# Two mask copies of the gated attention on ScalarE, and the root iterations of both norm tails on GpSimd

## The chip, the cores and the metric

One NeuronCore of a Trainium2 chip runs the kernel. Time is device microseconds (us) of one launch on that core; the number compared is the median of several runs. The engines are TensorE (PE in the profile, PEld for its weight loads), VectorE (DVE), ScalarE (ACT), GpSimd (POOL) and SyncE (SP), which issues most transfers. Each engine takes its own instructions strictly in order and waits for the others through semaphores.

## The reference, cut to what matters

One encoder layer runs over a prompt of 1024 frames and a sample of 64 frames, in float32. The change touches the two attentions and the norm that follows each of them.

```python
def _head_groupnorm(o):                      # after retention
    mu = jnp.mean(o, axis=-1, keepdims=True)
    var = jnp.mean(jnp.square(o - mu), axis=-1, keepdims=True)
    return (o - mu) * lax.rsqrt(var + EPS)

def _head_rms(o):                            # after gated linear attention
    return o * lax.rsqrt(jnp.mean(o * o, axis=-1, keepdims=True) + EPS)

def _gla(q, k, v, log_a, s0):
    ...
        rel = jnp.where(causal, b[:, :, :, None, :] - b[:, :, None, :, :], -jnp.inf)
        att = jnp.einsum('bhtd,bhsd,bhtsd->bhts', qc, kc, jnp.exp(rel))
        o = inter + jnp.einsum('bhts,bhse->bhte', att, vc)
...
    o_r = _merge(_head_groupnorm(o_r)) * g_ret_norm.astype(f32) * jax.nn.silu(rg)
    o_g = _merge(_head_rms(o_g)) * g_gla_norm.astype(f32) * jax.nn.silu(gr)
```

## The kernel before

The 1088 frames are cut into three column blocks of 384, 384 and 320, each of up to three groups of 128 frames. All projections are made as three float32r products (high by high, low by high, high by low) that accumulate in a PSUM tile called `mm`. First comes the head of the program (norm, conditioning, first projections), then the gated attention (two passes, one for each pair of heads, about 120 to 330 us), then retention (four heads, about 345 to 600 us), then the output projection and the ConvFFN, which the change leaves alone.

**The gated attention.** `gla(p, c0)` goes through the three blocks of one head pair. I call the work of one block a *stretch*; six of them follow one another. A stretch fills the score tile `att`, of which there is one buffer, in seven levels (`LEVELS` = 64, 32, 16, 8, 4, 2, 1) after a diagonal step. For a level of width c, `pre1` has GpSimd subtract (`dd`) and ScalarE take exponentials, `pre2` makes `kk` (GpSimd or VectorE) and `qbd` (VectorE), and `fin` has TensorE multiply them into a PSUM tile `sc` of two buffers, from which VectorE copies the valid part into `att` under an integer mask `tmask` (`copy_predicated`). After the levels come three outputs: TensorE makes `o` from `att`, the values and the state `sbd`; VectorE updates `sbd`, which the next output needs; ScalarE copies `o` into `on` and sums its squares.

**The tails.** When a block's outputs are out, a tail is started as a side task: `gla_tail` scales `on` by the reciprocal root of the mean square, transposes it on TensorE and writes it into `mix`. `ret_tail` does the same for a retention head and block, with mean and variance from `bn_stats`. The reciprocal root is made from integer tricks and three Newton iterations by `rsqrt_steps`, on VectorE: two integer operations and nine small operations on 128 x 6 (gated, tiles `ga`, `gr`) or 128 x 3 elements (retention, `ra`, `rr`). There are 6 gated and 12 retention tails. `ons` has one buffer in the gated attention and two in retention.

**What sets the order.** Nothing reorders instructions on the chip. While the program is written out, a planner keeps a model clock (`Flow`, `flow.t`) that each matmul moves forward, and side tasks (generators: `gla`, `ret`, the tails, `mod_pieces`) are resumed when the clock has passed their due time. `Engine` keeps a modelled backlog of each engine (`behind()`); a level's `pre1` waits while GpSimd or ScalarE is more than `LEVEL_LIMIT` behind, and `mod_pieces` (multiply-adds `acc` of the conditioning weights, off to the side) go in whenever VectorE is less than `VECTOR_LIMIT` behind. So a change in how much work an engine is charged moves levels, tails and `acc` operations to other places between the projection matmuls. When the projections that a pass has are used up, `flow.drain` lets the clock jump, and what is left of the pass is written with no projections in between.

Of the kernel before, what the change touches and what calls it, by code (L numbers as in the profile page):

```python
# [12 lines left out]
F32 = mybir.dt.float32  # L13
F32R = mybir.dt.float32r
I32 = mybir.dt.int32
AF = mybir.ActivationFunctionType
ALU = mybir.AluOpType
PSUM = bass.MemoryType.PSUM

P = 128  # L20
# [4 lines left out]
CW = 384  # L25
# [168 lines left out]
def stream_step_kernel(  # L194
# [130 lines left out]
                actp.tile([P, CW], F32R, tag="act", name="act_lo"))  # L325

    smallp = [small]

    def rsqrt_steps(v, n, tag, out, w=P):
        ii = smallp[0].tile([P, n], I32, tag=tag + "i", name=tag + "i", bufs=2)[0:w]  # L330
# [413 lines left out]
    op = order.op  # L744
# [195 lines left out]
    def gla(p, c0):  # L940
# [66 lines left out]
        def fin(c, o):  # L1007
            q, k = qk[p, "q"][c], qk[p, "k"][c]
            if o == "diag":
                for hd in range(2):  # L1010
                    r = slice(hd * 64, hd * 64 + 64)
                    pd = bank(ps_sc, "sc")
                    for j in range(3):
                        sl = slice(j * P, (j + 1) * P)
                        mm(pd[:, sl], k[r, sl], q[r, sl], True, True)
                    V.copy_predicated(
                        out=att[:, :, hd, :],
                        mask=tmask[:, 0:P][:, None, :].broadcast_to([P, 3, P]),
                        data=pd[:, 0:CW].rearrange("p (j t) -> p j t", t=P))
            elif o == "kh":  # L1020
                kh = live.pop((c, "kh"))
                pk = bank(ps_sc, "sc")
                for j in range(3):
                    tr(pk[:, j * P:(j + 1) * P], kh[:, j * P:(j + 1) * P])
                khT = live[c, "khT"] = attn.tile([P, CW], F32, tag="kT", name="khT", bufs=2)
                S.copy(out=khT, in_=pk[:, 0:CW])
            elif isinstance(o, int):
                cc = LEVELS[o]
                kk, z = live.pop((c, "z", o))
                pl = bank(ps_sc, "sc")  # L1030
                for j in range(3):
                    mm(pl[:, j * P:(j + 1) * P], kk[:, j * P:(j + 1) * P],
                       z[:, j, :, :].rearrange("p h t -> p (h t)"), True, True)
                ao = att.rearrange("p j h (n two t) -> p (j h) n two t", two=2, t=cc)
                mo = 128 + 64 * o
                V.copy_predicated(
                    out=ao[:, :, :, 1, :],
                    mask=tmask[:, mo:mo + 64].rearrange("p (n t) -> p n t", t=cc)[:, None, :, :]
                    .broadcast_to([P, 6, 64 // cc, cc]),
                    data=pl[:, 0:CW].rearrange("p (g n t) -> p g n t", g=6, t=cc))  # L1040
            elif o != "qe":
                j = o[1]
                if j == 0:
                    live[c, "on"] = (ons.get(),
                                     small.tile([P, 6], F32, tag="gss", name="gss", bufs=2))
                on, ss = live[c, "on"]
                v, qe, khT, eL = vts[c0][c], live[c, "qe"], live[c, "khT"], live[c, "eL"]
                gi = c * 3 + j
                sst = cur["s"] if gi < 8 else sbd[2]
                sl = slice(j * P, (j + 1) * P)  # L1050
                po = bank(ps_o, "o")
                pst = po[:, 256:512]
                if sst is not None:
                    mm(po[:, 0:256], qe[:, sl], sst.rearrange("p h e -> p (h e)"), True, False)
                for hd in range(2):
                    mm(po[:, hd * P:(hd + 1) * P], att[:, j, hd, :], v[:, j, hd * P:(hd + 1) * P],
                       sst is None, sst is None or hd == 1)
                mm(pst, khT[:, sl], v[:, j, :], True, True)
                ns = sbd[gi % 2]
                for hd in range(2):  # L1060
                    r = slice(hd * 64, hd * 64 + 64)
                    if sst is None:
                        V.tensor_copy(out=ns[r, hd, :], in_=pst[r, hd * P:(hd + 1) * P])
                    else:
                        V.scalar_tensor_tensor(out=ns[r, hd, :], in0=sst[r, hd, :],
                                               scalar=eL[r, j:j + 1],
                                               in1=pst[r, hd * P:(hd + 1) * P], op0=ALU.mult,
                                               op1=ALU.add)
                S.copy(out=on[:, j, :, :], in_=po[:, 0:256])
                for hd in range(2):  # L1070
                    junk = small.tile([P, P], mybir.dt.bfloat16, tag="junk", name="junk", bufs=2)
                    S.activation(out=junk, in_=on[:, j, hd, :], func=AF.Square,
                                 accum_out=ss[:, 2 * j + hd:2 * j + hd + 1])
                cur["s"] = ns
                if gi >= 7:
                    dst = o_gla_p if gi == 7 else o_gla_s
                    for hd in range(2):
                        nc.sync.dma_start(out=dst[0, 0, 2 * p + hd],
                                          in_=ns[hd * 64:hd * 64 + 64, hd, :])
                if j == 2:  # L1080
                    vs.free()
                    tails_.append(flow.start(gla_tail(p, c, on, ss), 1.0))
# [37 lines left out]
    def gla_tail(p, c, on, ss):  # L1120
# [1 line left out]
        ms = small.tile([P, 6], F32, tag="ms", name="ms", bufs=2)  # L1122
        V.tensor_scalar(out=ms, in0=ss, scalar1=1.0 / P, scalar2=EPS, op0=ALU.mult, op1=ALU.add)
        rs = []
        for _ in rsqrt_steps(ms, 6, "g", rs):
            yield 0.2
        rs = rs[0]
        yield 0.2
        for j in range(3):
            for hd in range(2):  # L1130
                i = 2 * j + hd
# [167 lines left out]
    def ret_tail(hd, c, on, mv):  # L1299
        w = WID[c]  # L1300
        ve = small.tile([P, 3], F32, tag="ve", name="ve", bufs=2)
        V.tensor_scalar(out=ve, in0=mv[:, :, 1], scalar1=EPS, scalar2=None, op0=ALU.add)
        rs = []
        for _ in rsqrt_steps(ve, 3, "r", rs):
            yield 0.2
        rs = rs[0]
        yield 0.2
        for j in range(3):
            V.tensor_scalar(out=on[:, j, :], in0=on[:, j, :], scalar1=mv[:, j, 0:1],
                            scalar2=rs[:, j:j + 1], op0=ALU.subtract, op1=ALU.mult)  # L1310
        yield max(V.behind(), 0.0) + RET_TAIL
        pt = bank(ps_sc, "sc")
        for j in range(3):
            tr(pt[:, j * P:(j + 1) * P], on[:, j, :])
        mt = mix[c][hd]
        if mt is None:
            S.activation(out=new_mix(c, hd)[:, 0:w], in_=pt[:, 0:w], func=AF.Copy,
                         scale=vec("gret", hd))
        else:
            V.scalar_tensor_tensor(out=mt[:, 0:w], in0=pt[:, 0:w], scalar=vec("gret", hd),  # L1320
                                   in1=mt[:, 0:w], op0=ALU.mult, op1=ALU.mult)
        rons.free()
        ready[c] += 1
# [1033 lines left out]
```

## Time and profile before

| | |
|---|---|
| median of 3 runs | 1491.79 us (1491.54 to 1493.49) |
| the profiled execution | 1496.77 us, of which 1495.0 us are its span |
| mean granted TensorE clock | 0.97 of full speed |
| busy share PE / DVE / ACT / POOL | 92% / 72% / 42% / 21% |
| gated attention, 120 to 345 us | PE busy 195.98 of 225 us |
| retention, 345 to 612 us | PE busy 243.64 of 267 us |

The profile shows one execution, read by the hardware profiler, with its own time; it is 5.0 us above the median of the three runs. "Busy" counts an instruction from start to end, with what it waits inside. An idle time is given with the instruction of another engine whose end released it. L91 is the line of the planner's helper that issues every VectorE, ScalarE and GpSimd operation, and L234 and L239 issue the matmuls and the transposes, so tiles tell the groups apart.

### The profile page before, as it was taken

What the parts mean: (1) busy time and instruction counts of PE and PEld (TensorE: products, weight loads), DVE (VectorE), ACT (ScalarE), POOL (GpSimd) and SP (SyncE); (2) the same over time, 40 slices, a digit from 0 to 9 for tenths busy, and PEclk for the clock granted to TensorE, in tenths of its full rate; (3) what the DMA queues carried; (4) which work ended last, traced back from release to release, by engine and by line L of the source; (5) the groups of instructions that cost most, each with busy time, mean ns of one, the idle gap of its engine ahead of it and who ended that gap; (6) DMA issues with size and microseconds to landing.
All of it is one profiled execution on the core that took longest, in us unless ns stands there. A gap on an engine that the chain in (4) does not pass through costs nothing.

```text
span 1495.0 us, 23802 instructions
## 1 busy us (share of the span) xinstructions
PE 1372.2 (92%) x9082; PEld 1277.3 (85%) x9082; DVE 1070.9 (72%) x1992; ACT 625.8 (42%) x1277; POOL 307.2 (21%) x412
## 2 busy tenths in 40 slices
PE   5999888989999998799779999999999999899996
PEld 3788777879988988798769999999999997788875
DVE  6637878967886788646697777777777765568775
ACT  5735434432333223435464444444434444334343
POOL 3335423415242323411110000000000011110010
PEclk9999999999999999899889999999999999999998
DMA  8420102123222222444302422333233338565522
GB/s 255 155 76 4 55 15 75 45 84 100 83 79 86 76 75 62 118 149 139 104 15 72 140 60 76 107 106 98 95 99 106 106 100 289 185 195 184 173 81 113
DMA packets 157977, 158.27 MB, mean 106 GB/s; under 512 B 9738, under 2 KB 128616, under 8 KB 157864
## 3 DMA queue, kind: packets, MB, share of 16 engines
q1 hardware_dynamic: 147303, 120.58, 26.1%
q0 software_dynamic: 10560, 36.18, 7.1%
q8 instruction: 71, 1.16, 0.3%
q14 instruction: 43, 0.34, 0.1%
HBM read 126.80 MB, written 29.93 MB: 105 GB/s over the span
## 4 chain that ended last, share of the span: by engine, by line
PE 56%; DVE 22%; issue 8%; ACT 6%; DMA 2%; POOL 1%; DVEq 0%; ACTq 0%; POOLq 0%
PE dX L234 23%; PE mm L234 10%; PE dA L234 8%; PE mn L234 5%; PE al L234 3%; PE o L234 2%; DVE lo L91 2%; DVE qbd L91 2%; DMA rb<-d_y 2%; DVE acc L91 2%; DVE att L91 1%; ACT hi L91 1%; DVE X L91 1%; PE sc L234 1%; DVE ab L91 1%
## 5 line engine op out<-in xcount | busy, mean ns | idle before, releaser
L234 PE MATMUL dX<-X,lo 128*128 128x272 f32 x1344 | 182.0, 292 | 5.5 <-DVE ab L91 3.4
L234 PEld LDWEIGHTS dX<-X,lo 128*128 128x128 f32 x1344 | 175.6, 191 | 6.6 <-ACT cv L91 3.0
L234 PE MATMUL dX<-X,hi 128*128 128x272 f32 x1296 | 174.8, 291 | 5.0 <-DVE ab L91 2.8
L234 PEld LDWEIGHTS dX<-X,hi 128*128 128x128 f32 x1296 | 168.7, 191 | 5.8 <-issue 2.9
L234 PE MATMUL mm<-act_hi,hi 128*128 128x384 f32 (+1 forms) x480 | 170.8, 356 | 0.3 <-DVE mix L91 0.2
L234 PE MATMUL mm<-act_lo,hi 128*128 128x384 f32 (+1 forms) x480 | 158.9, 331 | 0.1
L234 PE MATMUL mm<-act_hi,lo 128*128 128x384 f32 (+1 forms) x480 | 158.5, 330 | 0.0
L91 ACT CAST hi<-raw 128x512 fp32r<-128x512 f32 (+1 forms) x116 | 91.1, 787 | 78.9 <-DVE raw L91 66.7
L234 PE MATMUL al<-ba,hi 128*128 128x512 f32 x396 | 102.1, 401 | 4.8 <-DVE x L91 4.8
L234 PE MATMUL mn<-lo,hi 128*128 128x512 f32 x396 | 94.6, 395 | 2.7 <-ACT lo L91 2.1
L234 PEld LDWEIGHTS mm<-act_hi,hi 128*128 128x128 f32 x480 | 92.1, 192 | 1.9 <-DVE mix L91 0.5
L234 PEld LDWEIGHTS mm<-act_lo,hi 128*128 128x128 f32 x480 | 91.9, 191 | 0.7 <-POOL act_lo L91 0.3
L234 PEld LDWEIGHTS mm<-act_hi,lo 128*128 128x128 f32 x480 | 91.4, 190 | 0.0
L234 PEld LDWEIGHTS mn<-lo,hi 128*128 128x128 f32 x396 | 74.7, 190 | 19.4 <-ACT lo L91 2.6
L91 DVE SCALAR_TENSOR_TENSOR cv<-ab,cw,cv 128x1088 f32<-128x1088 f32 x44 | 59.3, 1347 | 44.3 <-ACT cv L91 44.3
L234 PEld LDWEIGHTS al<-ba,hi 128*128 128x128 f32 x396 | 72.3, 191 | 20.0 <-DVE x L91 5.9
L234 PE MATMUL mm<-hi,act_hi 128*128 128x256 f32 x288 | 88.3, 307 | 0.3 <-ACT hi L91 0.2
L234 PE MATMUL mm<-lo,act_hi 128*128 128x256 f32 x288 | 82.7, 287 | 3.0 <-DVE lo L91 3.0
L234 PE MATMUL mm<-hi,act_lo 128*128 128x256 f32 x288 | 82.1, 285 | 0.0
L91 POOL TENSOR_TENSOR acc<-acc,prod 128x512 f32<-128x512 f32 x42 | 64.8, 1544 | 81.6 <-ACT prod L91 80.8
L234 PE MATMUL dA<-X,hi 128*128 128x272 f32 x552 | 74.3, 291 | 0.0
L234 PEld LDWEIGHTS dA<-X,hi 128*128 128x128 f32 x552 | 71.8, 191 | 0.0
(352 smaller groups left out, 3091.7 us busy)
## 6 DMA issues: line engine op xcount, KB each, us to landing
raw<-in_w_ffn_in_dram SPq DMA_DIRECT2D x44, 512.0 KB
raw<-in_w_ada_dram SPq DMA_DIRECT2D x32, 512.0 KB
raw<-in_w_in_dram SPq DMA_DIRECT2D x28, 512.0 KB
rw<-in_w_ffn_out_dram SPq DMA_DIRECT2D x51, 256.0 KB
d_y<-cv POOLq DMA_DIRECT2D x22, 512.0 KB, 4.8
rb<-d_y POOLq DMA_DIRECT2D x44, 256.0 KB, 3.8
raw<-in_w_out_dram SPq DMA_DIRECT2D x18, 512.0 KB
wa<-in_w_ada_dram SPq DMA_DIRECT2D x16, 512.0 KB
```

The costliest lines, as they stand in the source:

```text
L91: return call(*args, **kw)
L234: T.matmul(out, lhsT, rhs, start=start, stop=stop, skip_group_check=more)
```

## The change

Two things change in `gla` and the tails. For the two widest levels, `fin` no longer calls `copy_predicated` on VectorE: ScalarE copies the valid rectangles, which need no mask (one copy of 64 x 6 x 64 elements for width 64, two of 32 x 6 x 32 for width 32). And both tails use `root_steps` instead of `rsqrt_steps`: the two integer operations stay on VectorE, back to back, and each of three iterations is four GpSimd operations in place of three on VectorE. The tails yield 0.5 between iterations (0.2 between single operations before), and afterwards until the modelled GpSimd backlog is over.

```diff
+    def root_steps(v, n, tag, out):
+
+        def part(name, dt=F32, bufs=2):
+            return small.tile([P, n], dt, tag=tag + name, name=tag + name, bufs=bufs)
+
+        ii, jj = part("i", I32), part("j", I32)
+        V.tensor_scalar(out=ii, in0=v.bitcast(I32), scalar1=1, scalar2=None,
+                        op0=ALU.logical_shift_right)
+        V.tensor_scalar(out=jj, in0=ii, scalar1=-1, scalar2=0x5F3759DF,
+                        op0=ALU.mult, op1=ALU.add)
+        r = jj.bitcast(F32)
+        G.after(V)
+        for it in range(3):
+            yield
+            a = part("a")
+            G.tensor_tensor(out=a, in0=r, in1=r, op=ALU.mult)
+            G.tensor_tensor(out=a, in0=a, in1=v, op=ALU.mult)
+            G.tensor_scalar(out=a, in0=a, scalar1=-0.5, scalar2=1.5, op0=ALU.mult, op1=ALU.add)
+            r2 = part("r", bufs=3)
+            G.tensor_tensor(out=r2, in0=r, in1=a, op=ALU.mult)
+            r = r2
+        out.append(r)
@@ in gla, fin(c, o), one of the levels
+                if o < 2:
+
+                    for n in range(64 // cc):
+                        r = slice(2 * cc * n, 2 * cc * n + cc)
+                        S.copy(out=att[r, :, :, 2 * cc * n + cc:2 * cc * (n + 1)],
+                               in_=pl[r, 0:CW].rearrange("p (j h t) -> p j h t", j=3, h=2)
+                               [:, :, :, cc * n:cc * (n + 1)])
+                    return
                 ao = att.rearrange("p j h (n two t) -> p (j h) n two t", two=2, t=cc)
@@ in gla_tail (and the same in ret_tail, with ve, 3 and "r")
-        for _ in rsqrt_steps(ms, 6, "g", rs):
-            yield 0.2
+        for _ in root_steps(ms, 6, "g", rs):
+            yield 0.5
         rs = rs[0]
-        yield 0.2
+        yield max(G.behind(), 0.2)
```

The order of the instructions moves with it. On TensorE, the end of the last gated stretch: the last level (`qbd`, `kk`), then the outputs (`sbd` with `qe`, `v` with `att`, `v` with `khT`), with projection matmuls (`mm`) among them. Before:

```order
L234 MATMUL sc<-qbd_1079,kk 128x128 x3
L234 MATMUL mm<-act_hi,hi 128x384
L234 MATMUL mm<-act_lo,hi 128x384
L234 MATMUL mm<-act_hi,lo 128x384
L234 MATMUL o<-sbd_1083,qe 128x256
L234 MATMUL o<-v,att 128x128 x2
L234 MATMUL o<-v,khT 128x256
L234 MATMUL mm<-act_hi,hi 128x384
L234 MATMUL mm<-act_lo,hi 128x384
L234 MATMUL mm<-act_hi,lo 128x384
L234 MATMUL o<-sbd_1081,qe 128x256
L234 MATMUL o<-v,att 128x128 x2
```

Now, from the same level to the tail's transposes (`sc<-ident,on`):

```order
L234 MATMUL sc<-qbd_1079,kk 128x128 x3
L234 MATMUL o<-sbd_1083,qe 128x256
L234 MATMUL o<-v,att 128x128 x2
L234 MATMUL o<-v,khT 128x256
L234 MATMUL o<-sbd_1081,qe 128x256
L234 MATMUL o<-v,att 128x128 x2
L234 MATMUL o<-v,khT 128x256
L234 MATMUL o<-sbd_1085,qe 128x256
L234 MATMUL o<-v,att 128x128 x2
L234 MATMUL o<-v,khT 128x256
L234 MATMUL st<-ident,acc_2927 128x128 x4
L239 MATMUL sc<-ident,on 128x128 x6
```

Before, projections stand between the outputs, and 45 more of them between the last output and the tail's transposes; now there are none in either place. They stand further ahead, in the earlier stretches.

On VectorE, in the second retention head: between the outputs' updates (`rstate`, `on`, `bst`, `bmv`) stand the root iterations of the tail one block back (`ra`, `rr`), and `on<-on,bmv,rr` ends it. Before:

```order
L91 SCALAR_TENSOR_TENSOR rr<-ra,rj 128x3
L91 SCALAR_TENSOR_TENSOR ra<-ve,rr 128x3
L91 TENSOR_TENSOR ra<-ra,rr 128x3
L91 SCALAR_TENSOR_TENSOR rr<-ra,rr 128x3
L91 SCALAR_TENSOR_TENSOR rstate<-rstate,o 128x128
L91 SCALAR_TENSOR_TENSOR on<-o,txi,on 128x128
L91 BN_STATS bst<-on 128x6
L91 BN_AGGR bmv<-bst 128x2
L91 SCALAR_TENSOR_TENSOR ra<-ve,rr 128x3
L91 SCALAR_TENSOR_TENSOR acc_4357<-raw,csil,acc_4357 128x512
L91 TENSOR_TENSOR ra<-ra,rr 128x3
L91 SCALAR_TENSOR_TENSOR rr<-ra,rr 128x3
```

Now, at the same place, up to the end of the tail:

```order
L91 TENSOR_TENSOR mix<-mix,gate 128x384
L91 SCALAR_TENSOR_TENSOR acc_4532<-raw,csil,acc_4532 128x512
L91 SCALAR_TENSOR_TENSOR rstate<-rstate,o 128x128
L91 SCALAR_TENSOR_TENSOR on<-o,txi,on 128x128
L91 BN_STATS bst<-on 128x6
L91 BN_AGGR bmv<-bst 128x2
L91 TENSOR_SCALAR on<-on,bmv,rr 128x128 x3
L91 TENSOR_TENSOR ratt<-sc,tdec 128x384
```

The small operations are gone from VectorE. On GpSimd, they now stand between the additions `acc<-acc,prod` of a conditioning piece, each of which waits for a product that ScalarE makes:

```order
L91 TENSOR_TENSOR acc_4533<-acc_4533,prod 128x512
L91 TENSOR_TENSOR ra<-rj 128x3
L91 TENSOR_TENSOR ra<-ra,ve 128x3
L91 TENSOR_SCALAR ra<-ra 128x3
L91 TENSOR_TENSOR rr<-rj,ra 128x3
L91 TENSOR_TENSOR acc_4533<-acc_4533,prod 128x512
```

Before, GpSimd had only the additions there.

## Rows read from the trace of the kernel before

**Rows 1.** Windows: length; PE, PEld, DVE, ACT, POOL busy; clock; DMA share, GB/s.

```profile
131.50:165.30 33.80, 27.75 (x174) 26.01 (x173) 28.50 (x53) 10.73 (x32) 14.46 (x14) 0.90 0.16 48
165.30:196.10 30.80, 26.09 (x166) 23.37 (x165) 24.12 (x52) 12.90 (x44) 12.80 (x13) 1.00 0.11 35
196.10:229.50 33.40, 29.25 (x190) 26.59 (x189) 28.35 (x57) 14.23 (x51) 11.64 (x14) 0.95 0.09 25
229.50:260.40 30.90, 25.96 (x193) 24.51 (x192) 25.24 (x55) 11.47 (x39) 12.62 (x14) 0.94 0.17 50
260.40:289.90 29.50, 26.86 (x197) 24.66 (x196) 26.51 (x55) 13.64 (x47) 11.64 (x12) 1.00 0.17 53
289.90:331.00 41.10, 35.65 (x218) 32.17 (x217) 30.01 (x69) 17.01 (x55) 12.38 (x12) 0.96 0.27 85
361.00:612.00 251.00, 229.68 (x1560) 222.23 (x1558) 188.86 (x479) 84.56 (x174) 85.59 (x71) 0.97 0.24 73
```

**Rows 2.** Waits, 120 to 345 us: total, times, longest.

```profile
PE sc L234 <- DVE att L91: 13.5, 11, 3.7
...
PE o L234 <- DVE sbd L91: 3.4, 9, 0.6
```

**Rows 3.** Waits, 345 to 610 us.

```profile
PE sc L239 <- DVE on L91: 10.2, 5, 3.1
...
PE o L234 <- DVE rstate L91: 4.1, 4, 1.5
```

**Rows 4.** Groups, VectorE, 120 to 345 us (roots: first, last of six).

```profile
L91 DVE COPY_PREDICATED att<-tmask,sc 128x384 f32<-128x384 int32 x54 | 35.9, 677 | 8.2 <-PE sc L234 7.4
...
L91 DVE SCALAR_TENSOR_TENSOR gr<-ga,gr 128x6 f32<-128x6 f32 x12 | 4.9, 407 | 0.4
...
L91 DVE SCALAR_TENSOR_TENSOR gr<-ga,gj 128x6 f32<-128x6 f32 x6 | 1.7, 290 | 0.0
```

**Rows 5.** Groups by form, ScalarE, 120 to 345 us.

```profile
L91 ACT COPY khT<-sc 128x384 f32<-128x384 f32 x6 | 2.9, 479 | 7.3 <-PE sc L239 7.3
```

**Rows 6.** Groups, VectorE, 345 to 610 us (first, last of six).

```profile
L91 DVE SCALAR_TENSOR_TENSOR ra<-ve,rr 128x3 f32<-128x3 f32 x24 | 6.9, 288 | 0.7
...
L91 DVE SCALAR_TENSOR_TENSOR ra<-ve,rj 128x3 f32<-128x3 f32 x12 | 2.7, 221 | 0.4
```

**Rows 7.** Timeline, VectorE, 440 to 453 us: a retention tail.

```profile
440.71 0.16 DVE L91 TENSOR_SCALAR ve<-bmv 128x3 f32<-128x3 f32 x1
...
446.43 1.15 DVE L91 SCALAR_TENSOR_TENSOR rr<-ra,rj 128x3 f32<-128x3 f32 x1
...
452.03 0.85 DVE L91 TENSOR_SCALAR on<-on,bmv,rr 128x128 f32<-128x128 f32 x3
```

**Rows 8.** Timeline around 171 us: start, duration, instruction.

```profile
171.09 1.21 DVE L91 TENSOR_TENSOR lo<-raw,hi 128x1024 fp32r<-128x1024 f32 x1
171.10 2.07 POOL L91 TENSOR_TENSOR qe<-qe,q 128x384 f32<-128x384 f32 x1
```

**Rows 9.** Groups by form, GpSimd, whole run.

```profile
L91 POOL TENSOR_TENSOR acc<-acc,prod 128x512 f32<-128x512 f32 x42 | 64.8, 1544 | 81.6 <-ACT prod L91 80.8
...
L91 POOL COPY tails<-ab 128x2 f32<-128x2 f32 x44 | 7.3, 217 | 100.9 <-DVE ab L91 100.9
```

**Rows 10.** Chain that ended last, a run of projection matmuls.

```profile
283.54 1.57 PE mm L234 x9
```

**Rows 11.** Timeline, 321 to 330 us: the last gated tail.

```profile
321.97 0.72 DVE L91 SCALAR_TENSOR_TENSOR sbd<-sbd,eL,o 64x128 f32<-64x128 f32 x2
...
323.91 0.17 DVE L91 TENSOR_SCALAR ms<-gss 128x6 f32<-128x6 f32 x1 [1.22 <-ACT junk L91]
...
328.75 1.86 ACT L91 ACTIVATE on<-on,gr 128x128 f32<-128x128 f32 x6 [2.81 <-DVE gr L91]
...
329.20 0.33 PE L239 MATMUL sc<-ident,on 128*128 128x128 f32 x1 [0.77 <-ACT on L91]
```

**Rows 12.** Windows around 450 us.

```profile
450.00:460.00 10.00, 7.42 (x47) 6.98 (x48) 8.49 (x33) 2.30 (x5) 0.70 (x1) 0.83 0.21 61
```

## What I expect of the change

> **What bounds the kernel now.** I read the windows first, cut at the start of each stretch of the gated attention. TensorE takes its work in a fixed order and the amount of that work does not change here, so in these phases time is lost only where TensorE stands idle, or runs at its lower clock. In [rows 1] idle is length less PE busy: 6.05, 4.71, 4.15, 4.94, 2.64 and 5.45 us in the six stretches, 27.9 us together, and 21.3 us in the retention row. VectorE is busy 24 to 28 us in each of the first five stretches, 78 to 90% of their length; ScalarE and GpSimd are below half. The waits say the same: in the gated attention the largest wait of TensorE is for `att`, 13.5 us in 11 pieces, and before each output it waits 0.38 us on average for the state `sbd` [rows 2]. In retention it is the tail's transposes, which wait 10.2 us in 5 pieces for `on`, and then `rstate` with 4.1 us [rows 3]. All of these are VectorE's products. So taking work off VectorE can pay, up to some 49 us if all idle time went, and whatever takes projections away from under these waits costs.
>
> **The change part by part.**
>
> *Mask copies.* 12 of the 54 `copy_predicated` go (two in each stretch). Their mean is 677 ns [rows 4], so 8.1 us of VectorE's time, 1.35 a stretch. ScalarE gets 18 copies, none larger than the 128 x 384 copy from PSUM at 479 ns [rows 5]: at most 8.6 us, 1.4 a stretch, on an engine that is busy 10.7 to 14.2 us in stretches of 30 [rows 1]. I count them as hidden. If that cover is gone (ScalarE waits for the level's matmul with the exponentials of a later level queued behind the copy), one copy costs its 0.48 us, 6 us in the worst case.
>
> *Root iterations, VectorE's side.* Nine operations in each of 18 tails go: 54 gated ones in six groups from 4.9 to 1.7 us, together 19.5 us [rows 4], and 108 retention ones in six groups from 6.9 to 2.7 us, together 26.7 us [rows 6]. Much of this is not work. `rr` at 446.43 takes 1.15 us where an undisturbed operation of that size takes 0.16, as `ve` does [rows 7], because it stands behind a GpSimd operation; how that happens is seen best at 171 us, where VectorE's `lo` and GpSimd's `qe` start together, `lo` takes 1.21 us and `qe`, 0.01 us later, 2.07 us [rows 8]: one runs, and the other holds. So 9 x 0.16 = 1.4 us a tail is certain to be saved on VectorE, and the rest only if no other VectorE operation inherits the wait.
>
> The Trainium skill, page "SBUF — State Buffer", section "Who interferes with whom", states it as a rule: a VectorE instruction with two SBUF inputs and a GpSimd instruction that reads SBUF shut each other out for the whole instruction. The pair at 171 us agrees. By this rule the iterations don't leave the contested port, they only change sides, and that speaks against the change; its result is the third rival below.
>
> *Root iterations, GpSimd's side.* 216 operations come, 12 in a chain for each tail. The trace of before has no arithmetic of 3 or 6 elements on GpSimd. The nearest row is the copy of 2 elements at 217 ns; the far end is the addition of 512 elements at 1544 ns, of which a good part is waiting [rows 9]. I take 0.22 us, since size is what the two rows differ in: 2.6 us a tail, against 1.4 to 1.8 us on a free VectorE. If each operation first had to wait out a VectorE operation of about 0.4 us, it would be 7 us a tail. Behind the chain are queued, on GpSimd, the next level's `dd`, for which ScalarE waits, and in retention the additions of a conditioning piece.
>
> *What moves.* This is the larger part, and the order shows it. The planner now charges GpSimd for the tails and holds levels back while it is behind, so levels stand further apart and more projection matmuls go between them. From the start of one stretch to that of the next, the order has 93, 78, 102, 99, 108 `mm` before and 99, 102, 90, 117, 135 now. One costs 1.57/9 = 0.174 us [rows 10]. The first two stretches of each pass get 6, 24, 18 and 27 more, 75 x 0.174 = 13 us of cover over 18.3 us of idle. A first wait of 3.7 us [rows 2], which is the first stretch's first level, stands ahead of every tail and stays; each output keeps its 0.38 us, and these stretches become limited by TensorE (28.8 to 31.6 us of its work, busy time plus added `mm`, against VectorE's 24 to 28). I leave 5.5, 2.6, 2.5 and 1.7 us, 12.3 together: -6.0 us.
>
> The third stretch of each pass pays for it. In the first pass its levels and outputs have 39 `mm` where they had 69: 30 x 0.174 = 5.2 us of cover lost. VectorE's queue there gets shorter by two copies (1.35 us) and nine roots (1.4), and longer by two reductions of 128 x 512 from PSUM that moved in, which I price like the masked copies (1.35), so 1.4 us comes back: +3.8 us. In the last stretch there is no projection after the transposes of `kh`: 18 `mm` fewer up to the last output, 3.1 us, and VectorE has six more `acc` there, which net of the copies and roots makes it 1.0 us longer: +4.1 us. And the last tail lies bare. Before, 45 `mm` (7.8 us) covered the time from the last `sbd` at 321.97 to the transposes at 329.20, 7.2 us [rows 11]. Between `ms` at 323.91 and the scaling at 328.75 lie 4.8 us with other work mixed in; two integer operations and 12 x 0.22 make 3.2. So 5.6 us remain, of which the 0.45 us of one set of transposes and the 1.3 us that was waited there already come off: +3.9 us. Together +8.0 us. The gated attention as a whole: -6.0 + 3.8 + 8.0 = +5.8 us.
>
> VectorE also gets to its conditioning work earlier: before the first retention scores the order has 54 `acc` operations on VectorE instead of 41, one whole piece more. This is why its load in the stretches hardly falls. In return, the last retention head has no piece beside it any more.
>
> *Retention.* The tail from `ve` at 440.71 to `on` at 452.03 takes 11.3 us [rows 7], and its transposes wait 3.1 us, the longest of the five [rows 3]; their place in TensorE's order is nearly the same now. The new chain is 0.5 us of VectorE, 2.6 us of GpSimd and one or two additions of 1.5 us between, 5 to 7 us, while VectorE's own queue up to `on` is 9 x 0.16 plus one to three waits of 1 us shorter. I take it that 6.5 of the 10.2 us go. The last head, with no `acc` on VectorE, loses its quarter of the 4.1 us for `rstate` and about as much for `ratt`, 2 us: -8.5 us.
>
> *Clock.* After the 3.1 us wait the granted clock reads 0.83 in the window from 450 [rows 12], that is, 1.7 us lost in 10 to the lower level (1.2 instead of 2.4 GHz). I count three such windows behind the five waits. I let two of them go and one new one come in the bare last stretch: -1.7 us.
>
> **Sum.** 5.8 - 8.5 - 1.7 = -4.4 us, against the profiled 1496.8 us: 1492.4. That execution is 5.0 us above the median of the runs, so the median becomes 1487.4 us; I say 1487 us. Its own range, with the terms a third off, is 1481 to 1493.
>
> **The rivals.**
>
> *Slower: the bare third stretches.* If VectorE's queue takes as long in them as before, since its next operations inherit the roots' waits, nothing of the lost cover comes back: 5.2 in the first pass, and in the second 3.1 and the 1.0 of the longer queue, a further 3 us because all 57 projections stand ahead of the fourth level, and the bare tail with a slow chain, 7 us. The two third stretches then cost 19 instead of 12 us; if the earlier stretches also keep half of their idle (-3 instead of -6) and the clock is a wash, it is +16 - 8.5 = +7.5 us, 1499 us. For it: VectorE is busy 28.35 of 33.4 us there [rows 1]. Against: part of that is waiting for GpSimd. It decides where these stretches and the tail cost 16 us, as much as the other three terms of the forecast give back (6.0 + 8.5 + 1.7).
>
> *Faster: the waits were VectorE's own.* If the removed roots take their blocked time with them (3.25 us a gated tail instead of 1.6), the third stretches cost 5 us instead of 12, and retention loses 9 us of waits for `on`, 2 in the last head and three clock windows: -6 + 5 - 11 - 5 = -17 us, 1475 us. For it: the groups' means of 221 to 407 ns stand well above 0.16 us [rows 4, 6]. Against: the next operation on VectorE may inherit the wait.
>
> *The iterations change sides only.* Each GpSimd operation waits for a VectorE operation, the chain is 7 us or more, `on` waits for GpSimd, and VectorE stands still behind it, with `rstate` and `ratt` queued there. Then retention gains nothing, and the gated +5.8 us remain: about 1498 us. It decides at a chain of 8 us.
>
> *Gain hidden.* The transposes' waits go, but TensorE meets the same lateness one wait further, at `ratt` and `rstate` (4.1 us for the latter before [rows 3]), so that retention yields 4 us instead of 8.5: about 0 us, 1492 us.
>
> **How the numbers follow.** What this kernel's measurement can tell from no change is about 0.2%, 3 us. Chances: the forecast 0.42, the bare stretches 0.18, the faster case 0.17, the hidden gain 0.14, the change of sides 0.09. Of the forecast's own range some seven tenths lie more than 3 us below 1491.8 and nearly all of the rest within it; with the faster case that makes 0.48 faster; the hidden gain and that rest make 0.25 the same; the two slower cases 0.27. For 8 in 10 the range has to reach into both outer cases: 1476 to 1499 us.
>
> **What would show it.** Right: the third stretch of the second pass has an idle of over 10 us, with waits for `on` before the last tail's transposes; the first two stretches of each pass are down to 2 to 3 us (the very first to 5 or 6); the wait of the transposes for `on` in retention falls below 4 us; a GpSimd root operation takes 0.2 to 0.25 us. Wrong: GpSimd roots of 0.5 us or more on average, VectorE waiting for `rr` in most retention tails, or waits for ScalarE's `att` copies on TensorE above 3 us, which would mean that the copies are not hidden.

## The result, and the profile after

The changed kernel takes 1531.56 us (median of four runs, 1529.42 to 1533.35) where the kernel before takes 1491.66 (1491.24 to 1493.49): 1.0263 of it, 95% interval 1.0247 to 1.0279. That is slower, by 40 us, and far outside the predicted range of 1476 to 1499 us. The profiled execution took 1529.42 us with a span of 1527.6 us, 32.6 us longer than the profiled span of before, which was one of its longer executions.

The windows of the changed kernel, cut at the same events as [rows 1] (the six stretches of the gated attention, the last one here up to the first scores of retention), and then all six together. Columns as in [rows 1].

```profile
132.00:166.90 34.90, 27.83 (x179) 26.00 (x178) 28.05 (x51) 11.73 (x36) 14.64 (x13) 0.95 0.16 47
166.90:210.30 43.40, 34.13 (x191) 30.80 (x190) 27.12 (x49) 14.27 (x48) 17.98 (x25) 0.88 0.16 49
210.30:248.10 37.80, 29.42 (x187) 26.72 (x186) 26.02 (x53) 14.72 (x49) 14.63 (x29) 0.82 0.12 34
248.10:280.40 32.30, 26.12 (x203) 24.26 (x202) 24.35 (x41) 12.68 (x45) 18.68 (x24) 1.00 0.22 66
280.40:320.00 39.60, 35.34 (x231) 32.70 (x230) 28.85 (x51) 17.79 (x54) 17.48 (x26) 0.96 0.14 41
320.00:392.60 72.60, 55.45 (x321) 51.80 (x321) 47.69 (x82) 20.33 (x60) 31.93 (x47) 0.88 0.26 80
132.00:392.60 260.60, 208.29 (x1305) 192.28 (x1305) 182.07 (x322) 91.52 (x290) 115.33 (x163) 0.91 0.19 56
```

The same of the kernel before, in one window, and its sixth stretch up to the first scores of retention ([rows 1] ends it at 331):

```profile
131.50:361.00 229.50, 198.44 (x1297) 183.77 (x1297) 187.75 (x369) 87.42 (x275) 94.03 (x92) 0.96 0.19 57
289.90:361.00 71.10, 62.53 (x384) 58.62 (x384) 55.03 (x102) 24.46 (x65) 30.86 (x25) 0.98 0.29 89
```

The gated attention is 31.1 us longer, which is nearly all of the 32.6. TensorE is idle for 52.3 instead of 31.1 us (length less PE busy), so 21.2 us are waiting. The other 9.9 us are PE busy time, with 762 projection matmuls in either kernel; eight matmuls of the extra conditioning piece are the only ones more. The granted clock says why: 0.91 instead of 0.96.

What TensorE waits for in the gated attention, and then in retention (engine, line, what it waited for: us, times, longest):

```profile
PE sc L239 <- DVE att L91: 9.4, 4, 4.1
PE sc L239 <- ACT on L91: 7.8, 4, 6.0
PE sc L239 <- ACT att L91: 7.0, 3, 3.5
PE o L234 <- DVE att L91: 7.0, 6, 2.5
PE sc L234 <- DVE att L91: 6.1, 3, 3.7
```

```profile
PE sc L239 <- DVE on L91: 17.1, 10, 4.8
```

Levels' matmuls wait less for `att` than in [rows 2] (6.1 instead of 13.5 us), but transposes (L239), which use the same two `sc` banks, now wait 9.4 us for VectorE's and 7.0 us for ScalarE's copies, and the last gated tail 6.0 us for `on`. In retention the transposes wait 17.1 us in 10 pieces, against 10.2 in 5 [rows 3]. The prediction had said that waits of over 3 us for ScalarE's `att` copies would mean that the copies are not hidden, and that was my first reading: ScalarE's copies stand in its queue behind exponentials, these wait for GpSimd, and GpSimd is busy with roots. In the second stretch the timelines of ScalarE and then VectorE look just like it (start, duration, instruction, idle before it and what ended it):

```profile
174.92 0.53 ACT L91 ACTIVATE kh<-kh 128x384 f32<-128x384 f32 x1 [6.11 <-POOL kh L91]
175.35 0.46 ACT L91 COPY att<-sc 64x384 f32<-64x384 f32 x1
...
183.93 1.23 DVE L91 TENSOR_TENSOR lo<-raw,hi 128x1024 fp32r<-128x1024 f32 x1 [6.32 <-ACT hi L91]
```

The experiments began with that theory of the engines' queues and one rival: that the loss is in the order of the instructions, TensorE's above all, which the planner's new charges changed.

### The profile page after: what moved, and what is told of

Read it like the earlier page. It is cut to its first block, busy times and chain, and to the rows that moved or that the text cites. A ratio compares the mean times of both kernels' runs of the same rounds, so it can differ in the third digit from the quotient of the medians.

```text
span 1527.6 us, 23819 instructions
## 1 busy us (share of the span) xinstructions
PE 1378.9 (90%) x9082; PEld 1281.4 (84%) x9082; DVE 1037.7 (68%) x1827; ACT 626.9 (41%) x1286; POOL 352.8 (23%) x620
## 4 chain that ended last, share of the span: by engine, by line
PE 50%; DVE 16%; ACT 6%; issue 6%; POOL 3%; DMA 2%; SPq 0%; DVEq 0%; ACTq 0%; POOLq 0%
PE dX L234 21%; PE mm L234 9%; PE dA L234 8%; PE mn L234 5%; PE al L234 3%; DVE lo L91 2%; DMA rb<-d_y 2%; DVE ab L91 1%; ACT hi L91 1%; PE o L234 1%; DVE cv L91 1%; DVE on L91 1%; DVE X L91 1%; PE sm L234 1%; ACT cv L91 1%
## 5 line engine op out<-in xcount | busy, mean ns | idle before, releaser
L91 DVE TENSOR_TENSOR lo<-raw,hi 128x1024 fp32r<-128x1024 f32 x43 | 54.5, 1268 | 28.5 <-ACT hi L91 28.2
```

Source lines behind the costliest of these rows:

```text
L91: return call(*args, **kw)
```

## The experiments

All ratios are to the kernel before, run on the same chip beside the experiment.

**The order apart from the engines.** `order_only` keeps the new charges and so TensorE's order instruction for instruction, but lets VectorE do the copies and iterations as before, without charging it:

```
+            for _ in range(4):
+                G.busy = max(G.busy, flow.t) + G.fixed + n / G.rate
...
-            G.tensor_tensor(out=a, in0=r, in1=r, op=ALU.mult)
...
+            nc.vector.scalar_tensor_tensor(out=a, in0=v, scalar=-0.5, in1=r, op0=ALU.mult,
+                                           op1=ALU.mult)
...
+                        S.busy = max(S.busy, flow.t) + S.fixed + 6 * cc / S.rate
-                V.copy_predicated(
+                (nc.vector if o < 2 else V).copy_predicated(
```

> TensorE's order, and the planner's charges, are those of the changed kernel; the two widest levels are copied by VectorE with the mask and the roots run on VectorE, as before. If the new order is the cause, this is slow too, 1515 to 1535 us. If the cause is where the copies and roots run (ScalarE's queue behind exponentials that wait for GpSimd), the time returns most of the way: 1485 to 1500 us, with the wait of ScalarE's kh and dd for GpSimd back near the 4.9 and 16.8 us of before.

`engines_only` is the reverse: ScalarE copies and GpSimd iterates, but the planner is charged as if VectorE did it, at the old points of the program, so that TensorE's order is that of before.

```
+    def vec_cost(n):
+        V.busy = max(V.busy, flow.t) + V.fixed + n / V.rate
...
+            vec_cost(n)
+            nc.gpsimd.tensor_tensor(out=a, in0=r, in1=r, op=ALU.mult)
...
+                        nc.scalar.copy(out=att[r, :, :, 2 * cc * n + cc:2 * cc * (n + 1)],
...
+                    V.busy = max(V.busy, flow.t) + V.fixed + CW / V.rate
```

> TensorE's order is that of before instruction for instruction (the planner is charged as if VectorE did the work), but ScalarE copies the two widest levels and GpSimd iterates the roots. If the cause is the coupled queues of GpSimd and ScalarE, this is slow: 1510 to 1530 us, with TensorE waiting over 10 us for sc buffers and att copies of ScalarE. If the new order is the cause, 1485 to 1495 us.

Measured: `order_only` 1.0233 (1.0201 to 1.0264), `engines_only` 1.0010 (0.9991 to 1.0028). As the account of the loss, the theory of the queues falls. The new order makes the loss with the old engines too, and the new engines cost nothing that can be measured in the old order. First `order_only`, the gated attention in one window and its second stretch, then `engines_only`, the gated attention:

```profile
132.00:384.60 252.60, 210.13 (x1306) 194.37 (x1305) 201.47 (x388) 85.61 (x272) 94.86 (x91) 0.90 0.19 58
167.81:205.63 37.82, 31.87 (x191) 28.71 (x190) 30.48 (x60) 13.14 (x45) 13.54 (x13) 0.95 0.18 56
```

```profile
130.10:365.30 235.20, 201.50 (x1298) 186.42 (x1298) 166.46 (x303) 93.81 (x293) 117.55 (x164) 0.95 0.18 55
```

The theory keeps a part inside the new order, though. With the old engines the second stretch takes 37.8 us instead of 43.4, and the gated attention 252.6 instead of 260.6. Behind the gated attention `order_only` is some 6 us the longer of the two, so that the whole times hardly tell them apart.

In `engines_only` VectorE has 21.3 us less to do than before (166.46 against 187.75), and the gated attention is no shorter. The waits of TensorE there show that the levels' wait for `att` has not moved from the 13.5 us of [rows 2]. VectorE's groups of `qbd` and `kk`, the products ahead of each level, show where the relief went (group: busy, mean ns | idle before, what ended it); first the kernel before, then `engines_only`:

```profile
PE sc L234 <- DVE att L91: 13.4, 9, 3.7
```

```profile
L91 DVE TENSOR_TENSOR qbd<-q,dd 64x192 f32<-64x192 f32 x84 | 36.6, 436 | 2.4 <-ACT dd L91 1.8
L91 DVE TENSOR_TENSOR kk<-k,dd 128x384 f32<-128x384 f32 x18 | 11.2, 622 | 0.0
```

```profile
L91 DVE TENSOR_TENSOR qbd<-q,dd 64x192 f32<-64x192 f32 x84 | 38.2, 454 | 9.6 <-ACT dd L91 7.6 <-POOL ga L346 1.4
L91 DVE TENSOR_TENSOR kk<-k,dd 128x384 f32<-128x384 f32 x18 | 11.6, 643 | 11.0 <-POOL gr L355 4.6 <-ACT dd L91 4.5 <-POOL ga L346 1.9
```

VectorE gets to these products earlier and waits there: before `qbd` 9.6 instead of 2.4 us, mostly for ScalarE's `dd`, and before `kk` 11.0 instead of none. It was busy for 78 to 90% of the first five stretches, but work taken off it did not make TensorE's inputs earlier. Part of the new idle time (4.6 us before `kk`) is VectorE waiting for the roots that went to GpSimd, so this run alone doesn't show that VectorE was not the bound. `copies_old_order` below adds no such wait: VectorE is busy 183.9 instead of 187.75 us, and the levels' wait for `att` is 13.0. That TensorE waits for a chain through GpSimd, ScalarE and VectorE is read from these rows; no run tests it by itself.

**The parts, with the planner charged for them.** `copies_only` and `gated_roots_only` are the change with one part alone.

> ScalarE copies the two widest levels, planner charged for it; roots on VectorE as before. If the loss is the copies alone, 1515 us or more. If it needs both (copies queued behind exponentials that wait for GpSimd, which is late because of the roots), at most a third of the 40 us: 1490 to 1505 us.

> Only the gated attention's roots iterate on GpSimd, planner charged for it; copies masked on VectorE and retention's roots on VectorE as before. If the roots alone make GpSimd late and with it ScalarE's exponentials, 1515 us or more. If the loss needs the copies as well, 1490 to 1505 us: kh and dd wait longer, but TensorE's sc buffers are emptied by VectorE all the same.

Measured: 1.0109 (1.0075 to 1.0142) and 1.0161 (1.0126 to 1.0195). Neither part is small alone. Their sum, 2.7%, is near the 2.6% of the whole change, but each has an order of its own, so this can be chance. `gated_roots_only` came out where the expectation had put the theory of the queues; the run of the same roots in the old order, below, shows that most of it is the order. Either charge is enough to move the order: the six stretches get 99, 84, 90, 114, 123 and 252 `mm` with the copies, 93, 102, 90, 114, 114 and 249 with the roots, where before had 93, 78, 102, 99, 108 and 282.

**The parts in the old order.** Three kernels with TensorE's order of before, in each one part of `engines_only`.

> TensorE's order as before; only the two widest levels' copies go to ScalarE, with the planner charged as before. If copies on ScalarE cost by themselves (a level waits for the sc buffer that ScalarE empties late), 1.003 or more of before. If they are hidden, as the prediction counted, 0.998 to 1.002.

> TensorE's order as before; only the gated roots iterate on GpSimd, planner charged as before. If they only change sides on the port, 1.000 to 1.004, with VectorE and ScalarE waiting for gr instead. If they free VectorE, as the prediction had it, 0.995 to 0.998.

> TensorE's order as before; only retention's roots iterate on GpSimd, planner charged as before. The prediction gave -6.5 us for the transposes' waits and some for the clock: 0.994 to 0.996. If VectorE then stands idle for rr (17.7 us in 7 pieces in the run with all three edits and the old order), the gain is smaller: 0.997 to 1.000, with waits of the transposes for on at 8 us or more.

Measured: copies 1.0003 (0.9981 to 1.0025), gated roots 1.0036 (1.0015 to 1.0056), retention's roots 1.0016 (1.0000 to 1.0031). The copies are hidden, as predicted. The gated roots cost a little by themselves. Retention's roots gain nothing, and the waits show why (TensorE's and VectorE's, in `rroots_old_order`):

```profile
PE sc L239 <- DVE on L91: 12.1, 12, 3.0
DVE on L91 <- POOL rr L355: 17.7, 7, 4.3
```

The two longest waits of [rows 3] did shrink, from 3.07 to 1.21 us, but tails that had not waited now do, so that 10.2 us in 5 pieces became 12.1 in 12. VectorE, which used to make the roots, now stands idle for `rr`, 17.7 us in 7 pieces. One of those two tails, from the timelines of VectorE and then of GpSimd:

```profile
444.70 0.16 DVE L91 TENSOR_SCALAR ve<-bmv 128x3 f32<-128x3 f32 x1
...
447.55 0.14 DVE L91 TENSOR_SCALAR rj<-ri 128x3 int32<-128x3 int32 x1
...
453.24 1.77 DVE L91 TENSOR_SCALAR on<-on,bmv,rr 128x128 f32<-128x128 f32 x3
...
449.23 0.19 POOL L355 TENSOR_TENSOR rr<-rj,ra 128x3 f32<-128x3 f32 x1
449.50 0.19 POOL L346 TENSOR_TENSOR ra<-rr 128x3 f32<-128x3 f32 x1
449.77 0.19 POOL L349 TENSOR_TENSOR ra<-ra,ve 128x3 f32<-128x3 f32 x1
450.00 1.28 POOL L91 TENSOR_TENSOR acc<-acc,prod 128x512 f32<-128x512 f32 x1
```

An iteration step takes 0.19 us but follows the one before it after 0.27, so twelve take 3.3 us, and an addition of 1.3 us stands between. From `ve` to `on` this tail takes 8.5 us instead of 11.3 [rows 7]; I had counted on 5 to 7. What I missed lies ahead of the chain: `rj` ends 3.0 us after `ve` starts, because other work of VectorE stands between, and I had taken 0.5 us for this.

**What in the order costs: the extra piece.** The changed order also brings one more conditioning piece into the gated attention, since VectorE, charged less, looks free to the planner. In `piece_held` the changed kernel stops VectorE's accumulations at the 32 of before until retention starts; `order_piece_held` does the same to `order_only`.

```
-                    while V.behind() > VECTOR_LIMIT or S.behind() > SCALAR_LIMIT:
+                    while V.behind() > VECTOR_LIMIT or S.behind() > SCALAR_LIMIT or \
+                            (phase[0] == "gla" and accs_done[0] >= 32):
```

> The changed kernel, with VectorE's conditioning work held at 32 accumulations until retention starts, as before (the change does 48 there). TensorE's order in the gated attention stays that of the changed kernel but for six mm. If the extra piece on VectorE is what the first two stretches of each pass lose by, 1510 to 1518 us; if it is the place of the projections (spent early, missing at the end), 1525 to 1533 us.

> TensorE's order of the changed kernel, with old engines for the copies and the roots, and VectorE's accumulations held at 32 until retention. If the extra piece costs about 12 us also with the old engines, 1.013 to 1.018; what is left then is the place of the projections alone. If the piece is all of it, 1.000 to 1.006; if it is nothing with the old engines, 1.021 or more.

Measured: 1.0182 (1.0146 to 1.0217) and 1.0128 (1.0088 to 1.0168). The expectation of `piece_held` set one cause against the other; it is both. Holding the piece back takes 0.8 and 1.0 points off the loss, 12 to 16 us. In the profiled executions the gated attention becomes 6.3 and 3.1 us shorter by it, retention 4.0 and 8.9. Some 1.3% remain that neither the engines nor the piece explain.

**What in the order costs: the place.** Two kernels are the one before with a single number of the planner changed, one is the changed kernel with two numbers loosened.

```
-LEVEL_STEP = 0.3
+LEVEL_STEP = 0.4
```

> The kernel before with one number of the planner changed: 0.4 instead of 0.3 us between levels. Engines, charges and the number of accumulations in the gated attention stay; the stretches get 93, 78, 108, 111, 126, 246 mm instead of 93, 78, 102, 99, 108, 282, and nothing stands any more between the last gated output and its tail. If projections spent early are missing at the end, this alone costs: 1.005 to 1.012, with idle and a lower granted clock in the sixth stretch. If the loss comes from the engines or from the extra piece, 0.998 to 1.002.

```
-LEVEL_LIMIT = 1.0
+LEVEL_LIMIT = 0.6
```

> The kernel before with one number of the planner changed: a level is held back while GpSimd or ScalarE is more than 0.6 instead of 1.0 us behind. Engines and charges stay. The stretches get 102, 96, 108, 108, 120, 228 mm and the extra piece comes into the gated attention, much as in the changed kernel. If holding levels back is by itself what costs, 1.015 to 1.025. If the loss needs the new charges or engines, under 1.008.

```
-LEVEL_LIMIT = 1.0
+LEVEL_LIMIT = 3.0
-LEVEL_LATE = 0.3
+LEVEL_LATE = -0.5
```

> The changed kernel with two numbers of the planner loosened: levels held back only over 3 us instead of 1, and scores sent 0.5 us before they are thought due instead of 0.3 after. Engines as in the changed kernel; the stretches get 93, 93, 90, 123, 117, 264 mm, with no extra piece, and 21 of the 45 mm stand again behind the last output. If the place of the projections and the extra piece are the cause, most returns: 1.002 to 1.010. If GpSimd's and ScalarE's queues cost in any new order, 1.015 or more.

Measured, in this order: 1.0191 (1.0157 to 1.0226), 1.0146 (1.0116 to 1.0177) and 1.0153 (1.0121 to 1.0184). With no engine and no charge touched, either number alone costs 1.5 to 1.9%. Neither run moves the place alone: `before_hold06` brings the extra piece in, and `before_step04` makes a piece late. `before_step04` came out above what I expected, and `after_loose` above what the theory of the place gave it and where the expectation had put the queues. The rows show other costs. First the gated attention of `after_loose`, then TensorE's longest wait behind retention and the transposes' waits in retention:

```profile
131.20:363.40 232.20, 201.27 (x1316) 189.86 (x1316) 159.59 (x294) 91.88 (x292) 111.85 (x165) 0.93 0.16 47
```

```profile
PE st L239 <- DVE acc L91: 19.2, 1, 19.2
PE sc L239 <- DVE on L91: 17.7, 9, 3.9
```

The same two of `before_step04`:

```profile
PE st L239 <- DVE msum L91: 10.8, 1, 10.8
PE sc L239 <- DVE on L91: 24.2, 8, 5.2
```

The gated attention of `after_loose` is back to 232.2 us, against 229.5 of before; but the last conditioning piece is now finished after retention is, and TensorE stands 19.2 us for it behind retention. In `before_step04` this wait is 10.8 us, and its gated attention is 10.2 us longer. The kernel before waits at that place for a load alone, 9.0 us, which these two don't, so the late piece costs some 10 and 2 us net. The transposes' waits for `on` grew as well, from 10.2 us to 17.7 and 24.2. So a piece can cost at either end: brought in early it cost 12 to 16 us, finished late up to 10.

**The clock.** In `order_piece_held` the gated attention has 5.9 us more idle time than before but 14.1 us more PE busy time:

```profile
132.40:381.90 249.50, 212.57 (x1298) 196.77 (x1298) 188.38 (x370) 87.05 (x274) 96.48 (x93) 0.88 0.17 52
```

To see whether the lower clock follows the waits or is something of its own, I filled waits with matmuls whose results nobody reads, in the changed kernel and in the one before:

```
+    def fill(n):
+        pd = bank(ps_st, "st")
+        for _ in range(n):
+            T.matmul(pd[:, 0:CW], h[0][0][1][:, 0:P], h[0][0][0], start=True, stop=True)
...
+            if (p, c, o) in FILL:
+                fill(FILL[p, c, o])
```

> The changed kernel with 142 matmuls more, 128x384, whose results nobody reads, put right ahead of ten instructions for which TensorE stood idle for 2 to 6 us in the changed kernel (first level, transposes of kh, one output, the last gated tail, three tails of retention). They do nothing but keep TensorE at work while it would wait. If the lower level of the clock follows from these waits, the granted clock of the gated attention rises from 0.91 to 0.96 or more and 6 to 12 us come back: 1519 to 1526 us in the terms of the 1531.6. If it has another cause, or the added work delays what comes behind, 1531 us or more.

> The kernel before with 74 such matmuls at its own seven longest waits (two first levels, two sixth levels behind a tail's transposes, three tails of retention), sized to about two thirds of each wait. In the profile of before the granted clock reads 0.50 to 0.70 for 3 to 7 us behind these seven, some 12 us of lost work in all. If the clock follows the waits, part of it comes back: 0.993 to 0.998. If not, 1.000 to 1.003.

Measured: 1.0183 (1.0157 to 1.0209) and 1.0015 (0.9996 to 1.0033). TensorE has 142 matmuls more and the changed kernel becomes some 12 us faster. Windows from 180 to 192.5 us, first of the changed kernel, then filled (the wait of 4.1 us for `att` lies there):

```profile
180.00:185.00 5.00, 1.79 (x8) 0.81 (x6) 1.07 (x1) 4.95 (x15) 0.80 (x2) 1.00 0.15 51
185.00:190.00 5.00, 2.29 (x9) 2.28 (x10) 4.96 (x9) 1.45 (x5) 3.81 (x4) 0.53 0.31 105
190.00:192.50 2.50, 2.50 (x12) 2.50 (x12) 0.88 (x4) 0.65 (x2) 0.21 (x1) 0.57 0.00 0
```

```profile
180.00:185.00 5.00, 3.77 (x21) 3.32 (x20) 3.35 (x5) 3.07 (x9) 1.23 (x2) 1.00 0.19 42
185.00:190.00 5.00, 4.59 (x32) 4.39 (x33) 4.96 (x8) 1.67 (x5) 4.19 (x5) 1.00 0.16 63
190.00:192.50 2.50, 1.79 (x12) 1.50 (x11) 2.44 (x6) 0.00 (x0) 1.37 (x2) 1.00 0.00 0
```

In the changed kernel the granted clock falls from 2.4 GHz to the lower of its two levels, 1.2 GHz, during the wait (0.53 and 0.57 on average), and the matmuls that come then run at half speed; with the wait filled it stays at 1.00. Over the gated attention it reads 0.97 instead of 0.91. The Trainium skill, page "TensorE: Matmul & The Clock Gate", section "HAM oscillation — how this bites in real kernels", describes a kernel that falls back to the lower level after each wait between its bursts and pays for it each time; these rows agree.

`before_fill` missed its gain. In its profile the gated attention is 4.4 us shorter and retention 2.4 us longer: two of its seven places were at tails that don't wait, and the two waits of 3.07 us were still there. With these put right, and then with ScalarE's copies in the old order besides:

> The kernel before with 68 matmuls nobody reads at its own seven longest waits: as in before_fill, but the two in retention that stood at tails without a wait now stand at the two that wait 3.07 us. In before_fill the gated attention came out 4.4 us shorter at a granted clock of 0.99 instead of 0.96. If that is the clock alone, the two tails in retention give 1.5 us each besides: 0.993 to 0.997. If the gain was chance, 0.999 to 1.002.

> The same 68 matmuls, and the two widest levels copied by ScalarE in the old order. If the copies are worth nothing by themselves, the same as before_fill2 within 0.2%. If a shorter VectorE queue and a full clock add, 0.3% less than it.

Measured: 0.9952 (0.9937 to 0.9968) and 0.9944 (0.9924 to 0.9964). Both beat the kernel before, by 7 to 8 us; the copies add nothing that can be told apart. It is the whole times that carry this. With the same fillings the gated attention took 225.1 us in the profile of `before_fill` and 228.3 in that of `before_fill2`, so one profile doesn't tell where the gain lies. The windows from 135 to 142.5 us, in the kernel before and then in `before_fill2`, show the first place, the wait of 3.7 us of [rows 2] and what follows it:

```profile
135.00:137.50 2.50, 0.10 (x1) 0.13 (x1) 2.46 (x4) 0.52 (x1) 2.21 (x3) 0.64 0.00 0
137.50:140.00 2.50, 2.50 (x12) 2.50 (x13) 1.75 (x5) 1.12 (x4) 1.62 (x3) 0.50 0.04 10
140.00:142.50 2.50, 2.50 (x14) 2.50 (x14) 1.25 (x3) 0.00 (x0) 0.26 (x1) 0.50 0.00 0
```

```profile
135.00:137.50 2.50, 2.50 (x18) 2.50 (x17) 2.46 (x6) 0.14 (x1) 1.31 (x2) 1.00 0.00 0
137.50:140.00 2.50, 1.57 (x11) 1.28 (x10) 2.44 (x6) 0.78 (x3) 1.77 (x2) 1.00 0.00 0
140.00:142.50 2.50, 2.50 (x24) 2.50 (x23) 2.47 (x4) 0.73 (x3) 1.97 (x2) 1.00 0.01 3
```

## Why the prediction was wrong

**The step that failed** is the cover: "The first two stretches of each pass get 6, 24, 18 and 27 more, 75 x 0.174 = 13 us of cover over 18.3 us of idle", from which it left 12.3 us. It set the sum of the added matmuls against the sum of the idle time, as if they stood at the waits. They don't. In the second stretch the changed order has 15, 15 and 24 `mm` ahead of the first three levels, ahead of which TensorE had waited 0.2 us in all (6, 6 and 6 before). The places that do wait kept what they had: 3 `mm` between a tail's transposes and what follows them (the sixth level before, the transposes of `kh` now), and 3 ahead of the first output. TensorE's timeline of the changed kernel at these two:

```profile
187.71 0.90 PE L239 MATMUL sc<-ident,kh 128*128 128x128 f32 x3 [4.13 <-DVE att L91]
...
202.30 1.17 PE L234 MATMUL o<-v,att 128*128 128x128 f32 x4 [2.53 <-DVE att L91]
```

So the idle time of these four stretches rose from 18.3 to 26.8 us, instead of falling to 12.3. The term was -6.0 us and should have been +8.5 in idle time alone. The new order with the old engines makes half of it (22.5 us idle in `order_only`); the other half needs the new engines in that order. The extra piece is not behind it: in `piece_held` the four stretches are idle for 26.9 us. Where the matmuls stand could have been read from the order alone.

**VectorE as the bound** was the reading behind it, and it did not hold. That TensorE's waits end on VectorE's products does not make VectorE the one that is late; `engines_only` took 21.3 us of work off it, and the 13.5 us of waits for `att` stayed at 13.4. What is late in its place is not shown beyond the waits for `dd` and `gr` above.

**The third stretches**, +3.8 and +8.0 us, were right in mechanism and size for what they counted, idle time: it rose from 4.15 to 8.38 and from 8.57 to 17.15 us, +4.2 and +8.6. The bare last tail waited 6.0 us for `on`, for which 5.6 was forecast. What they left out is the clock, 0.82 instead of 0.95 and 0.88 instead of 0.98 there. Counted by the change in length, with 0.174 us for each `mm` that the stretch gave up (12 and 63), the changed kernel lost 4.4 + 2.1 = 6.5 and 1.5 + 11.0 = 12.5 us, 19 instead of 12. That is the size that the slower rival had given them, but it had put it on VectorE's queue, so the agreement is luck. That rival still said 1499, since it too let the early stretches gain.

**The extra piece** was seen ("one whole piece more") and given no price in the sum. Held back, it is worth 12 to 16 us of the whole time; the terms above hold what it costs in the gated attention.

**Retention**, -8.5 us, gave nothing: from its first scores to the first matmul behind it, it takes 247.0 instead of 244.6 us. The transposes' waits for `on` grew to 17.1 us; they do so in `order_only` as well (17.5 us in 10 pieces), so it is mainly the order there too. In the old order the roots on GpSimd gain nothing, because VectorE then waits for `rr`. That is what the rival of the iterations that change sides had said of retention, though at a chain of 8 us; in the tail shown GpSimd's part took 5.4 us.

**The clock**, -1.7 us, had the wrong sign: 9.9 us more PE busy time in the gated attention alone. The term let one window of 1.7 us go; the waits grew instead, and each costs the matmuls behind it as well as its own length. With 8.5, 4.2 and 8.6 us of idle time, this makes up the 31.1 us of the gated attention.

**Right** were the price of a GpSimd step (0.19 to 0.20 us median, 0.22 taken), the copies as hidden in the old order, and the shape of the end. Of its signs of being wrong, TensorE's waits for ScalarE's `att` copies came (7.0 us), though the copies cost nothing measurable in the old order, and VectorE's waits for `rr` came in 6 of the 12 retention tails (17.1 us). One sum was slightly off: seven tenths of 0.42 and 0.17 make 0.46 faster, not 0.48. The rule of the port (the Trainium skill, page "SBUF — State Buffer", section "Who interferes with whom") bears most on `groots_old_order`: 0.36% slower, with `qbd`, which has two inputs in SBUF, at a mean of 488 instead of 436 ns. That agrees with a wait that other VectorE operations inherit; that it adds to the 40 us is not shown, since all the new engines together cost nothing measurable in the old order.

What stays open: which of the planner's rules spends the most (the limit on levels alone makes 1.5%, with the extra piece in it, the step alone 1.9%, with the late piece in it); how the remaining 1.3% of `order_piece_held` divide beyond what its rows show, 5.9 us more idle and 14.1 us more busy time at the lower clock; why, with the old engines, the extra piece costs more in retention than in the gated attention; and which of the new engines makes the second stretch longer in the new order.

## What to carry to other kernels

Where a planner's charges set the order, run a change of engine twice: new engines in the old order, and old engines in the new order. Set added cover against each wait by its place in the order, never sum against sum, and price work that the planner pulls forward as well as what it pushes out. A wait on TensorE may cost twice, once as idle time and once in the clock behind it; here matmuls that nobody reads, put at the longest waits, gave 0.5%.

## What the runs showed of the hardware

- A chain of GpSimd instructions of 128 x 3 or 128 x 6 elements takes 0.19 to 0.20 us for each in the median, and 0.27 to 0.29 us from one to the next where nothing else stands between; single ones took up to 0.69 us.
- Eight of TensorE's waits in the two attentions of the kernel before, of 2.0 to 3.7 us, were followed by 3 to 7 us of a granted clock of 0.50 to 0.70, but not every such wait was: behind a wait of 2.04 us at 181.66 us in the kernel before the clock stayed at 1.00, and behind one of 2.17 us at 211.80 it read 0.50 from 215.0 to 217.5.
- Matmuls that nobody reads held the clock up: 0.99 instead of 0.96 over the gated attention of the kernel before, which came out 4.4 and 1.2 us shorter in the two profiles. At a tail without a wait they cost their time, and one group waited 2.0 us itself, for `msum` to be read out of the bank that it writes.
